# A running log-sum-exp on one core: carry by a VectorE shuffle, own-row sums on GpSimd, nine matmuls a tile, a pipeline one stage deeper

## The chip, the core and the metric

The kernel runs on one core of a Trainium2 chip. The metric is device time in microseconds (us), the median of several executions. Most agree within 0.3% (one slow one is left out).

In these kernels TensorE does the matmuls, ScalarE (ACT in the profile) the exponentials and logarithms, VectorE (DVE) and GpSimd (POOL) the sums. The tiles lie in SBUF; the matmuls write to PSUM. SyncE (SP) issues the transfers. Each transfer is split over 16 DMA engines. In a line of a timeline the first two numbers are start and duration in us, and the bracket at the end gives the wait before it and what ended it.

## The reference

The input x is 4 x 4096 x 4128 in fp32. Along the second axis the output is a running log-sum-exp:

```
out[:, 0] = x[:, 0]
for t in 1..4095:
    mx = max(out[:, t-1], x[:, t])
    out[:, t] = mx + log(exp(out[:, t-1] - mx) + exp(x[:, t] - mx))
```

Both kernels compute exp(x), a running sum, and the logarithm of it.

## The kernel before

A tile is 128 partitions x 3 consecutive rows x 4128 columns (6.34 MB); 4096 rows are ten tiles of three rows and one of two, 44 tiles in all. The first batch starts with its two-row tile, the others end with theirs. A tile arrives by one load, is worked on in place, and leaves by one store. There are four tile buffers. The columns are worked on in four chunks of 1024 (the last takes the remaining 32 too):

```
own:        row j += row j-1, j = 1, 2                      (VectorE)
head:       above += excl^T @ row 2   (sums of the partitions above)   (TensorE)
add_above:  all rows += above         (PSUM operand)        (VectorE)
pick:       above = last partition's last row, for the next tile       (TensorE)
...
for g, k in enumerate(chunks):
    if g + 1 < len(chunks):
        chunks[g + 1].own();  chunks[g + 1].head()
    if g + 2 < len(chunks):
        chunks[g + 2].act(ACT.Exp)
    if g:
        finish(chunks[g - 1]);  result(chunks[g - 1])       # Ln; after the last chunk: store(s), load(s + 3)
    k.add_above()
    ...                                                     # pick
```

ScalarE takes its work in the order in which this loop issues it, so the place of `act(Exp)` says how far ahead ScalarE runs.

The softmax here doesn't subtract the row's maximum and nothing guards it: scores larger than these inputs give would overflow.

## Time and profile before

| | before |
|---|---|
| median time | 1263.7 us (1263.48 to 1264.46) |
| span of the profiled run | 1266.3 us |
| VectorE / ScalarE / TensorE / GpSimd busy | 981 / 924 / 760 / 1 us |
| one 6.34 MB store, issue to landing | 27.0 us |
| one 6.34 MB load, issue to landing | 41.1 us |

The profiled run was a slow one of its kind: other runs of this kernel have spans of 1261.7 to 1264.1, so differences taken from its trace are about 4 us too small. The two latencies are in the last column of the list of transfers:

```profile
xt<-in_x_dram SPq DMA_DIRECT2D x40, 6192.0 KB, 41.1
out_dram<-xt SPq DMA_DIRECT2D x40, 6192.0 KB, 27.0
```

What exceeds the transfer's own time is time in the queue.

### The profile page before, as it was taken

How to read it: one execution, taken by the hardware profiler on the slowest of the kernel's cores; microseconds unless marked ns; L12 is line 12 of the kernel's file. 1: busy time of each engine (PE TensorE's matmuls, PEld its weight loads, DVE VectorE, ACT ScalarE, POOL GpSimd, SP SyncE). 2: the span in 40 equal slices, each digit the busy share in tenths (PEclk: the TensorE clock that was granted, in tenths of full speed). 3: DMA queues.
4: the chain of work that ended last, by engine and by line, in shares of the span. 5: the costliest groups of instructions: out<-in, count | busy, mean ns of one | idle time of the engine just before them, and what ended most of it. 6: DMA issues, size and time to landing. Idle time of an engine off the chain costs nothing.

```text
span 1266.3 us, 4623 instructions
## 1 busy us (share of the span) xinstructions
PE 760.5 (60%) x1512; PEld 289.0 (23%) x1512; DVE 980.6 (77%) x597; ACT 923.8 (73%) x353; POOL 1.1 (0%) x8
## 2 busy tenths in 40 slices
PE   4676665555666666666366666665646656666562
PEld 1222222222222222222122222222212222222220
DVE  3998777777777878788579878777857978787793
ACT  4887666777777777767668777666866877766794
POOL 0000000000000000000000000000000000000000
PEclk9998888887788888888779888888877988888886
DMA  9999999999999999999999999999999999999998
GB/s 409 384 425 424 427 429 443 426 427 440 432 429 441 426 430 440 429 431 433 434 434 434 429 440 430 431 437 433 432 419 434 426 433 433 431 432 438 426 418 349
DMA packets 12695, 541.35 MB, mean 427 GB/s; under 512 B 1409, under 2 KB 1409, under 8 KB 1409
## 3 DMA queue, kind: packets, MB, share of 16 engines
q1 hardware_dynamic: 12672, 541.07, 99.3%
q8 instruction: 12, 0.20, 0.1%
q14 instruction: 11, 0.08, 0.0%
HBM read 270.53 MB, written 270.53 MB: 427 GB/s over the span
## 4 chain that ended last, share of the span: by engine, by line
DMA 67%; DVE 12%; ACT 9%; PE 8%; issue 1%; SPq 0%; ACTq 0%
DMA xt<-in_x_dram 63%; DVE xt L77 12%; ACT xt L106 9%; PE above L74 8%; DMA out_dram<-xt 5%; SPq L97 0%; ACTq L106 0%; SPq L94 0%; DVE carry_t L146 0%
## 5 line engine op out<-in xcount | busy, mean ns | idle before, releaser
L106 ACT ACTIVATE xt<-xt 128x3072 f32<-128x3072 f32 (+2 forms) x352 | 922.5, 2693 | 327.0 <-DMA xt<-in_x_dram 290.5
L74 PE MATMUL above<-xt,excl 128*128 128x512 f32 (+1 forms) x792 | 443.1, 687 | 348.7 <-DVE xt L77 339.4
L77 DVE TENSOR_TENSOR xt<-xt 128x1024 f32<-128x1024 f32 (+1 forms) x336 | 413.4, 1230 | 255.0 <-ACT xt L106 249.4
L77 DVE TENSOR_TENSOR xt<-xt,above 128x3072 f32<-128x3072 f32 (+3 forms) x220 | 582.9, 2651 | 11.7 <-PE above L74 10.3
L74 PE MATMUL above<-xt,pick 128*128 128x512 f32 x640 | 330.7, 630 | 130.0 <-DVE xt L77 130.0
L74 PEld LDWEIGHTS above<-xt,excl 128*128 128x128 f32 x792 | 162.6, 229 | 601.5 <-issue 490.5
L74 PEld LDWEIGHTS above<-xt,pick 128*128 128x128 f32 x640 | 113.6, 198 | 307.4 <-DVE xt L77 227.2
L74 PEld LDWEIGHTS above<-carry_t,pick 128*128 128x128 f32 x80 | 20.8, 271 | 51.4 <-DVE xt L77 48.2
L74 PE MATMUL above<-carry_t,pick 128*128 128x32 f32 x80 | 17.5, 308 | 10.1 <-DVE xt L77 10.1
L146 DVE COPY carry_t<-xt 32x32 f32<-32x32 f32 x40 | 7.1, 178 | 1.4
L56 ACT ACT_TABLE_LOAD x1 | 1.3, 1283 | 0.8 <-PEq L214 0.8
L69 DVE MEMSET carry_t<- 128x32 f32 x1 | 0.1, 85 | 0.9 <-PEq L214 0.9
L27 POOL TENSOR_SCALAR_AFFINE_SELECT pick<-pick 128x128 f32<-128x128 f32 x1 | 0.3, 293 | 0.0
L21 POOL TENSOR_SCALAR_AFFINE_SELECT excl<-excl 128x128 f32<-128x128 f32 x1 | 0.3, 292 | 0.0
L19 POOL MEMSET excl<- 128x128 f32 x1 | 0.2, 204 | 0.3 <-POOLq L214 0.3
L26 POOL MEMSET pick<- 128x128 f32 x1 | 0.2, 204 | 0.0
L214 POOL MEMSET const-bfloat16-1.0<- 128x1 bf16 x1 | 0.1, 101 | 0.0
L214 POOL MEMSET const-uint8-127<- 128x1 uint8 x1 | 0.1, 101 | 0.0
L214 POOL MEMSET const-float32-0.0<- 128x1 f32 x1 | 0.1, 98 | 0.3 <-issue 0.3
L214 POOL MEMSET const-float32-1.0<- 128x1 f32 x1 | 0.1, 98 | 0.0
## 6 DMA issues: line engine op xcount, KB each, us to landing
xt<-in_x_dram SPq DMA_DIRECT2D x40, 6192.0 KB, 41.1
out_dram<-xt SPq DMA_DIRECT2D x40, 6192.0 KB, 27.0
xt<-in_x_dram SPq DMA_DIRECT2D x4, 4128.0 KB, 36.2
out_dram<-xt SPq DMA_DIRECT2D x4, 4128.0 KB, 19.6
```

The costliest lines, as they stand in the source:

```text
L19: nc.gpsimd.memset(excl, 1.0)
L21: nc.gpsimd.affine_select(out=excl, in_=excl, pattern=[[1, P]], compare_op=mybir.AluOpType.is_ge, fill=0.0, base=-1, channel_multiplier=-1,)
L26: nc.gpsimd.memset(pick, 0.0)
L27: nc.gpsimd.affine_select(out=pick, in_=pick, pattern=[[0, P]], compare_op=mybir.AluOpType.not_equal, fill=1.0, base=-(P - 1), channel_mul ...
L56: nc.scalar.preload_act_table_set("natural_log_exp_and_others")
L69: nc.vector.memset(carry_t, 0.0)
L74: nc.tensor.matmul(pt, lhsT=w, rhs=rhs, start=start, stop=stop, skip_group_check=True)
L77: nc.vector.tensor_tensor(out=o, in0=a, in1=b, op=mybir.AluOpType.add)
L106: nc.scalar.activation(v, v, func)
L146: nc.vector.tensor_copy(carry_t[96:, :], t.xt[96:, t.r - 1, t0:D])
L214: nc = _bacc.Bacc("TRN2", target_bir_lowering=False, num_devices=1)
```

## The change

Its intent: take work off TensorE and VectorE. The last row's sum goes by a shuffle on VectorE into a small `carry` and is added to the next tile's first row (`begin`), so the `pick` matmuls and the accumulation in PSUM fall away. GpSimd does the own-row sums. The pipeline gets one stage deeper, four loads are issued at the start, and the last tile runs by itself after all others are done. The diff, cut:

```
+    carry = [psum.tile([Q, CH], ...)] + [cpool.tile([Q, ...]) for c in 1..3]      # Q = 32
+        def begin(self):
+            if not t.first:
+                nc.vector.scalar_tensor_tensor(out=v, in0=carry[c], scalar=one, in1=v, mult, add)
         def own(self):
-                add(v, x[:, j - 1, a:b], v)
+                add(nc.gpsimd, v, x[:, j - 1, a:b], v)
+        def end(self):
+            if not t.final:
+                nc.vector.stream_shuffle(carry[c], t.xt[P - Q:, t.r - 1, a:b], [Q - 1] * Q)
...
-    for s in steps[:ahead]:
+    for s in steps[:bufs]:
         s.load()
...
+    for part in (steps[:-1], steps[-1:]):
+        ...
+        for g in range(-3, N + 1):
+            chunks[g + 3].act(ACT.Exp)
+            chunks[g + 2].begin();  chunks[g + 2].own()
+            chunks[g + 1].head()
+            result(chunks[g - 1])                            # Ln, store, load
+            chunks[g].add_before();  chunks[g].end()
```

More of the change, by code (lines that the diff above doesn't have):

```diff
@@ L13 @@
 MM = 512
+Q = 32
 def _constants(nc, pool):
@@ L24, in _constants @@
     )
-    pick = pool.tile([P, P], FP32, name="pick")
-    nc.gpsimd.memset(pick, 0.0)
+    one = pool.tile([Q, 1], FP32, name="one")
+    nc.gpsimd.memset(one, 0.0)
     nc.gpsimd.affine_select(
-        out=pick, in_=pick, pattern=[[0, P]], compare_op=mybir.AluOpType.not_equal,
-        fill=1.0, base=-(P - 1), channel_multiplier=1,
+        out=one, in_=one, pattern=[[0, 1]], compare_op=mybir.AluOpType.not_equal,
+        fill=1.0, base=0, channel_multiplier=1,
     )
-    return excl, pick
+    return excl, one
 @with_exitstack
@@ L50 @@
     assert S % P == 0
-    n_main = D // CH
-    tail = D - n_main * CH
-    t0 = n_main * CH
-    last = n_main - 1
+    NC = D // CH
+    tail = D - NC * CH
+    t0 = NC * CH
+    last = NC - 1
     nc.scalar.preload_act_table_set("natural_log_exp_and_others")
     consts = ctx.enter_context(tc.tile_pool(name="consts", bufs=1))
-    excl, pick = _constants(nc, consts)
+    excl, one = _constants(nc, consts)
     bufs = 4
@@ L62, with add @@
     cpool = ctx.enter_context(tc.tile_pool(name="cpool", bufs=1))
+    hpool = ctx.enter_context(tc.tile_pool(name="hpool", bufs=2, space=bass.MemoryType.PSUM))
     psum = ctx.enter_context(tc.tile_pool(name="psum", bufs=1, space=bass.MemoryType.PSUM))
-    above = [psum.tile([P, CH], FP32, name=f"above{c}") for c in range(n_main)]
-    above_t = above[last][:, CH - MM:CH - MM + tail]
-    carry_t = cpool.tile([P, tail], FP32, name="carry_t")
-    nc.vector.memset(carry_t, 0.0)
+    carry = [psum.tile([Q, CH], FP32, name="carry0")]
+    carry += [cpool.tile([Q, CH if c < last else D - last * CH], FP32, name=f"carry{c}")
+              for c in range(1, NC)]
     ctx.enter_context(tc.manual_schedule())
-    def mm(pt, w, rhs, start=False, stop=False):
-        nc.tensor.matmul(pt, lhsT=w, rhs=rhs, start=start, stop=stop, skip_group_check=True)
-    def add(o, a, b):
-        nc.vector.tensor_tensor(out=o, in0=a, in1=b, op=mybir.AluOpType.add)
+    def add(eng, o, a, b):
+        eng.tensor_tensor(out=o, in0=a, in1=b, op=mybir.AluOpType.add)
     class Step:
@@ L106, in act @@
             nc.scalar.activation(v, v, func)
+        def begin(self):
+            t = self.t
+            if not t.first:
+                v = t.xt[:Q, 0, self.a:self.b]
+                nc.vector.scalar_tensor_tensor(
+                    out=v, in0=carry[self.c], scalar=one, in1=v,
+                    op0=mybir.AluOpType.mult, op1=mybir.AluOpType.add,
+                )
         def own(self):
@@ L112, in own, with add_before @@
                 v = x[:, j, self.a:self.b]
-                add(v, x[:, j - 1, self.a:self.b], v)
+                add(nc.gpsimd, v, x[:, j - 1, self.a:self.b], v)
         def head(self):
-            t, a = self.t, self.a
-            for s in range(0, CH, MM):
-                mm(above[self.c][:, s:s + MM], excl, t.xt[:, t.r - 1, a + s:a + s + MM],
-                   start=t.first, stop=True)
-        def add_above(self):
-            t, a = self.t, self.a
-            v = t.xt[:, :, a:a + CH]
-            add(v, v, above[self.c].unsqueeze(1).to_broadcast([P, t.r, CH]))
-        def pick(self, s0=0, s1=CH):
-            t, a = self.t, self.a
-            if not t.final:
-                for s in range(s0, s1, MM):
-                    mm(above[self.c][:, s:s + MM], pick, t.xt[:, t.r - 1, a + s:a + s + MM],
-                       start=True)
-        def tail_head(self):
-            t = self.t
-            if not t.first:
-                mm(above_t, pick, carry_t, start=True)
-            mm(above_t, excl, t.xt[:, t.r - 1, t0:D], start=t.first, stop=True)
-        def tail_add(self):
-            t = self.t
-            v = t.xt[:, :, t0:D]
-            add(v, v, above_t.unsqueeze(1).to_broadcast([P, t.r, tail]))
-            if not t.final:
-                nc.vector.tensor_copy(carry_t[96:, :], t.xt[96:, t.r - 1, t0:D])
+            t = self.t
+            e = t.xt[:, t.r - 1, self.a:self.b]
+            self.pt = hpool.tile([P, CH], FP32, name="pt")
+            parts = [(self.pt[:, s:s + MM], e[:, s:s + MM]) for s in range(0, CH, MM)]
+            if self.c == last:
+                self.qt = psum.tile([P, tail], FP32, name="qt")
+                parts.append((self.qt, e[:, CH:]))
+            for o, v in parts:
+                nc.tensor.matmul(o, lhsT=excl, rhs=v, start=True, stop=True)
+        def add_before(self):
+            t = self.t
+            parts = [(t.xt[:, :, self.a:self.a + CH], self.pt)]
+            if self.c == last:
+                parts.append((t.xt[:, :, t0:], self.qt))
+            for v, p in parts:
+                add(nc.vector, v, v, p.unsqueeze(1).to_broadcast(v.shape))
+        def end(self):
+            t = self.t
+            if not t.final:
+                nc.vector.stream_shuffle(
+                    carry[self.c], t.xt[P - Q:, t.r - 1, self.a:self.b], [Q - 1] * Q,
+                )
     steps = []
@@ L158 @@
         assert row == S
-    chunks = [Chunk(s, c) for s in steps for c in range(n_main)]
     ahead = bufs - 1
-    for s in steps[:ahead]:
+    for s in steps[:bufs]:
         s.load()
     stored = 0
-    def finish(k):
-        if k.c == last:
-            k.tail_add()
-            k.pick(CH - MM)
     def result(k):
@@ L174, in result @@
             k.t.store()
-            if stored + ahead < len(steps):
+            if bufs <= stored + ahead < len(steps):
                 steps[stored + ahead].load()
             stored += 1
-    chunks[0].act(ACT.Exp)
-    chunks[1].act(ACT.Exp)
-    chunks[0].own()
-    chunks[0].head()
-    for g, k in enumerate(chunks):
-        if g + 1 < len(chunks):
-            chunks[g + 1].own()
-            chunks[g + 1].head()
-        if g + 2 < len(chunks):
-            chunks[g + 2].act(ACT.Exp)
-        if g:
-            finish(chunks[g - 1])
-            result(chunks[g - 1])
-        k.add_above()
-        if k.c == last:
-            k.tail_head()
-            k.pick(0, CH - MM)
-        else:
-            k.pick()
-    finish(chunks[-1])
-    result(chunks[-1])
+    for part in (steps[:-1], steps[-1:]):
+        chunks = [Chunk(s, c) for s in part for c in range(NC)]
+        N = len(chunks)
+        for g in range(-3, N + 1):
+            if 0 <= g + 3 < N:
+                chunks[g + 3].act(ACT.Exp)
+            if 0 <= g + 2 < N:
+                chunks[g + 2].begin()
+                chunks[g + 2].own()
+            if 0 <= g + 1 < N:
+                chunks[g + 1].head()
+            if 0 <= g - 1:
+                result(chunks[g - 1])
+            if 0 <= g < N:
+                chunks[g].add_before()
+                chunks[g].end()
 _INS = ['x']
```

## The prediction

> **What bounds the kernel now.** I began with the page's slices and queues.
>
> ```profile
> DMA  9999999999999999999999999999999999999998
> GB/s 409 384 425 424 427 429 443 426 427 440 432 429 441 426 430 440 429 431 433 434 434 434 429 440 430 431 437 433 432 419 434 426 433 433 431 432 438 426 418 349
> ...
> q1 hardware_dynamic: 12672, 541.07, 99.3%
> ```
>
> The DMA row has no gap, and the queue's packets fill 99.3% of 16 engines' span. 541.07 MB is the input once and the output once, and the change moves the same bytes. Next, busy time by stretch, with three places where the slices dip:
>
> ```profile
> 100.00:1230.00 1130.00, 685.11 (x1355) 260.38 (x1356) 886.22 (x538) 832.26 (x314) 0.00 (x0) 0.87 1.00 432
> ...
> 42.00:100.00 58.00, 42.39 (x88) 15.40 (x86) 55.66 (x34) 49.00 (x19) 0.00 (x0) 0.94 0.98 401
> 42.00:44.50 2.50, 2.00 (x6) 0.72 (x5) 2.47 (x3) 2.50 (x2) 0.00 (x0) 1.00 0.50 211
> ...
> 1241.00:1266.30 25.30, 4.02 (x8) 1.70 (x8) 5.96 (x4) 7.97 (x5) 0.00 (x0) 0.59 0.89 386
> ```
>
> The last two columns are the DMA share and GB/s. Between 100 and 1230 us the rate is a flat 432; 541.07 MB at 432 is 1252.5 us. The span of 1266.3 is thus only about 14 us above a stream without a gap: some 4 us in 42 to 100 (58 x (1 - 401/432), with the hole at 42 in it), some 3 us at the start (403 GB/s over the first 42 us), the rest at the end.
>
> Then I asked how much slack feeds the stream: the timeline of the DMA-issuing queue and of ScalarE.
>
> ```profile
> 385.53 0.34 SPq L97 DMA_DIRECT2D out_dram<-xt  x1
> 385.96 0.38 SPq L94 DMA_DIRECT2D xt<-in_x_dram  x1
> 415.31 0.34 SPq L97 DMA_DIRECT2D out_dram<-xt  x1
> 415.75 0.38 SPq L94 DMA_DIRECT2D xt<-in_x_dram  x1
> ```
> ```profile
> 368.68 13.38 ACT L106 ACTIVATE xt<-xt 128x3072 f32<-128x3072 f32 x5 [7.11 <-DMA xt<-in_x_dram]
> 382.66 8.23 ACT L106 ACTIVATE xt<-xt 128x3168 f32<-128x3168 f32 x3 [0.61 <-PE above L74]
> ```
>
> A load lands, ScalarE wakes at 368.68, and the store of the tile before goes out at 385.53: C = 16.9 us from landing to next issue. With the store goes one load. Such a pair is 2 x 6.34 MB, so at 432 GB/s 29.4 us of transfer, which is the step between the pairs. A pair issued C after a landing finds 29.4 - 16.9 = 12.5 us still queued. The page agrees: its stores land a median 27.0 us after issue, 12.3 more than the 14.7 one takes. So C may grow by some 12 us before the stream starves, and shrinking it gains nothing.
>
> **What the Trainium skill says.** "DMA: Bandwidth & Descriptors", section Where 436 GB/s comes from, gives a ceiling of 435.2 GB/s for the 16 ports. The 432 over 1130 us agrees, so there is no rate to win. "GPSIMD Engine Reference", section 3.1, has the fp32 tensor_tensor add of 2048 elements at 4497 ns on GpSimd against 2293 on VectorE. The trace has VectorE's 1024 at 1222 ns, which fits; it has no such GpSimd work, so 2.3 us for 1024 is an estimate (half of 4497, rounded up). "VectorE: DVE Perf Modes", the perf-mode tier table, has the shuffle at one element a cycle, about 2400 ns for 2048: an estimated 1.2 us for 1024. "SBUF — State Buffer", section SBUF: two separate sides, says that a VectorE operation with two SBUF inputs and a GpSimd operation that reads SBUF exclude each other for whole instructions. No run yet shows that; nothing ran on GpSimd.
>
> **The change part by part.** From the groups by shape:
>
> ```profile
> L106 ACT ACTIVATE xt<-xt 128x3072 f32<-128x3072 f32 x240 | 645.9, 2750 | 273.0 <-DMA xt<-in_x_dram 273.0
> ...
> L77 DVE TENSOR_TENSOR xt<-xt,above 128x3072 f32<-128x3072 f32 x160 | 535.7, 3348 | 1.2
> ...
> L77 DVE TENSOR_TENSOR xt<-xt 128x1024 f32<-128x1024 f32 x252 | 308.1, 1222 | 248.3 <-ACT xt L106 244.0
> ```
>
> VectorE loses 336 own-row adds (413.4 us on the page) and the 40 small copies (7.1). It gains 160 adds of the carry into row 0 (32x1024, estimate 1.22, as a 1024 add: 195 us) and 160 shuffles (1.2: 192 us). 980.6 - 420.5 + 387 = 947 us: hardly less. GpSimd gets 336 x 2.3 = 773 us, 61% of the span. TensorE drops from 1512 matmuls to 44 x 9 = 396; at about 0.65 us for a 512-wide one it goes from 760 to some 250 us busy. ScalarE keeps 923. None reaches the span, so the stream stays the bound if C stays below 29.4.
>
> New C: exponentials now run three chunks ahead instead of two, so ScalarE does four exponentials and four logarithms between the landing and the store: 8 x 2.75 = 22 us. Do the others keep up? A chunk needs its carry add on VectorE (1.22), then two GpSimd adds (4.6), beside which VectorE does the add of the prefix (3.35) and a shuffle (1.2), 4.55. In three of four chunks the carry lies in SBUF, so the next carry add has two SBUF inputs and must wait for GpSimd: a chunk takes 1.22 + 4.6 + about 0.4 for handing over, 6.2 us, a tile 25 us. Under 29.4, and C stays 22, since the logarithm that ends it belongs to a chunk whose row sums were done before the landing. Queued at an issue: 29.4 - 22 = 7.4 us instead of 12.5. **In steady state the change buys and costs nothing.**
>
> Start: four loads go out at once, not three, which fills the hole at 42 (about 1.3 us lost: 2.5 x (1 - 211/432), near 2 us by packets). But ScalarE, behind since 27.7 us, sends the second store at about 27.7 + 4 x 4.65 + 22 = 68.3 or a little later, while four loads and the first store end near 4 x 14.7 - 4 + 10 + 2 = 67. A hole of the same kind moves there. I book -1 us.
>
> End: this is where the kernels differ. The chain of waits shows before's last tile:
>
> ```profile
> 1226.15 1.92 ACT xt L106
> ...
> 1246.34 2.30 DVE xt L77
> ...
> 1249.67 1.96 ACT xt L106
> ```
>
> The last load lands at 1226, its exponentials run while the tile before is finished, and the last store is issued at 1251.7, 4 us before the one ahead of it has gone out (the trace's landings: 1255.8, then 1265.5). So before's end is transfer. After drains the last-but-one tile before it starts the last. From its landing (1201.7) that tile needs 22 us, then two more rounds of row sums, prefix and logarithm, about 15: near 1238. Only then the last tile's exponentials: 1.9 + 1.2 for the first carry add, four chunks of GpSimd (2.3 each, with a 1.2 us carry add between, as the two exclude each other: 12.8), matmuls 2.2, add 2.5, logarithm 2: 22.6 us. Last store at about 1260.5, 9.8 us of transfer, then the 1 us that before has too: about 1271.5, +5 us. Without the exclusion 3.6 us less: +1.5.
>
> Sum: 1263.6 - 1 + 4 (between +1.5 and +5, nearer the upper) = 1266.6; I say 1266.
>
> **Rivals.** (a) GpSimd becomes the bound. Two adds and a carry add per chunk exceed 29.4/4 = 7.35 us if one add takes over 2.9 us. At 3.3 us with hand-over 0.4 a tile takes 4 x (1.22 + 6.6 + 0.4) = 33 us, 44 tiles about 1440. For it: no GpSimd add in the trace, only an estimate. Against: it would have to be 26% slower than the page's figure. (b) The exclusion reaches further than I think. If shuffles also shut GpSimd out, a chunk is 1.22 + 4.6 + 1.2 + 0.4 = 7.4 us, on the edge: 1270 to 1290. If every VectorE add does, it is above 10 us and the kernel above 1750. Against: the prefix add has one input in PSUM. (c) Freed VectorE, and TensorE no longer on the path, speed it up. The chain gives them 20% of the span, but the DMA row is full beside it: that chain is one thread of a closed loop whose spare 12 us show as queueing. Even with both dips removed it would be 1250 to 1255, inside 2%. (d) The end costs nothing, because the drained pipeline lets the last-but-one store go earlier: 1262.
>
> **Range and chances.** With the stream the bound, the time lies between 1258 (start and end both better) and 1277 (the exclusion at the end in full, its terms 5 us too small). For (a) and (b) together I give about 10% of being over 1289. Faster by over 2% means below 1238, under the 1252.5 of the stream itself: 1%.
>
> **What would show it.** Right: DMA still 9s everywhere, 432 GB/s from 100 to 1230, stores landing about 22 us after issue instead of 27, some 22 us from a landing to the next store, GpSimd near 770 us with adds of 2.3 us, and the loss in the last 40 us with a gap in the transfers before the last store. Wrong: 8s or less in the middle of the DMA row, ScalarE waiting for VectorE or TensorE instead of loads, GpSimd adds of 3 us or more, carry adds stretched far over 1.2 us, or a last store issued before 1252.

## The result, and the profile after

The changed kernel took 1294.78 us (1290.85 to 1295.14), 31 us more. The ratio is 1.0238, 95% interval 1.0217 to 1.0258. Ratios here are the mean time of one kernel's fast runs over that of the other's in the same rounds, so not quite the ratio of the medians. The forecast of 1266, with a range up to 1277, was wrong.

The page of the changed kernel, with its slices and its queue:

```profile
DMA  9999999999999999999999999999999999999987
GB/s 405 422 383 414 427 437 431 428 440 432 425 440 431 426 435 420 433 426 388 400 443 405 425 420 439 437 423 438 384 422 441 397 417 439 434 423 440 430 346 302
...
q1 hardware_dynamic: 12672, 541.07, 98.0%
```

The DMA row still looks full, but the row below it does not. The kernel before has one such dip near the start too (384; here 383) and one in its last slice (349). New are 388, 384 and 397 in the middle and 346 and 302 at the end. Busy time by stretch of the changed kernel (start and end, length, then PE, PEld, DVE, ACT and POOL; last three columns: granted TensorE clock, DMA share, GB/s):

```profile
594.00:602.00 8.00, 5.63 (x7) 1.85 (x6) 7.91 (x6) 5.85 (x3) 6.07 (x3) 0.50 0.65 279
42.00:100.00 58.00, 35.64 (x44) 11.97 (x44) 57.20 (x40) 47.51 (x18) 45.61 (x20) 0.59 0.95 388
100.00:1200.00 1100.00, 513.63 (x675) 179.99 (x676) 850.55 (x602) 792.98 (x301) 693.01 (x293) 0.61 0.99 425
1271.00:1284.00 13.00, 4.67 (x11) 1.80 (x10) 7.31 (x5) 6.46 (x4) 2.43 (x1) 0.76 0.33 142
```

The same question to the kernel before:

```profile
594.00:602.00 8.00, 6.04 (x13) 2.41 (x14) 7.85 (x6) 5.92 (x3) 0.00 (x0) 1.00 1.06 456
100.00:1200.00 1100.00, 666.59 (x1318) 253.00 (x1318) 861.17 (x522) 806.80 (x304) 0.00 (x0) 0.87 1.00 432
```

So 1100 us of stream went from 432 to 425 GB/s: the same bytes take 18 us longer. Around 594 to 602 us the engines move 279 GB/s where they moved 456. And near the end there are 13 us at 142.

Was it an engine that became the bound? The groups by shape say no:

```profile
L78 POOL TENSOR_TENSOR xt<-xt 128x1024 f32<-128x1024 f32 x252 | 596.2, 2367 | 421.9 <-DVE xt L114 368.4 <-ACT xt L107 44.1
L136 PE MATMUL pt<-xt,excl 128*128 128x512 f32 x704 | 590.4, 988 | 676.0 <-POOL xt L78 664.9 <-DVE xt L78 10.3 <-issue 0.8
...
L114 DVE SCALAR_TENSOR_TENSOR xt<-carry,one,xt 32x1024 f32<-32x1024 f32 x120 | 159.1, 1326 | 211.8 <-ACT xt L107 209.1
...
L149 DVE STREAM_SHUFFLE carry<-xt 32x1024 f32<-32x1024 f32 x120 | 152.4, 1270 | 1.6
```

A GpSimd add takes 2.37 us (2.3 had been estimated), a carry add 1.33 and a shuffle 1.27 (1.22 and 1.2). Only TensorE is far off: 600 us busy instead of 250. Its lines on the two pages, before and after:

```profile
PE 760.5 (60%) x1512; PEld 289.0 (23%) x1512; DVE 980.6 (77%) x597; ACT 923.8 (73%) x353; POOL 1.1 (0%) x8
PE 600.5 (46%) x792; PEld 210.1 (16%) x792; DVE 990.9 (77%) x700; ACT 920.9 (71%) x353; POOL 800.1 (62%) x344
```

The page lists two records for each matmul call: 792 for the 44 x 9 = 396 calls of the changed kernel, 1512 for 756 before. The forecast multiplied calls by the time of one record. On top of that a 512-wide record takes 988 ns at a granted clock of 0.62, not 650. All engines still wait often. The time from a landing to the next store is also as forecast. A load's last engine lands at 400.02; then ScalarE and the issuing queue:

```profile
400.05 21.50 ACT L107 ACTIVATE xt<-xt 128x3072 f32<-128x3072 f32 x8 [7.79 <-DMA xt<-in_x_dram]
```
```profile
421.57 0.33 SPq L98 DMA_DIRECT2D out_dram<-xt  x1
422.00 0.38 SPq L95 DMA_DIRECT2D xt<-in_x_dram  x1
```

Eight ScalarE instructions, 21.5 us, then the store: C, the time from landing to store, is 21.5 us where 22 was predicted. The queue shrank as predicted too:

```profile
xt<-in_x_dram SPq DMA_DIRECT2D x40, 6192.0 KB, 37.3
out_dram<-xt SPq DMA_DIRECT2D x40, 6192.0 KB, 22.8
```

What the forecast had not asked is whether all 16 DMA engines have that queue. The trace records when each of them finishes its share of a transfer. Here are first and last engine around the first inner two-row tile:

| transfer | before: first to last engine, us | after: first to last engine, us |
|---|---|---|
| load of tile 20 | 568.6 to 573.6 | 571.9 to 578.3 |
| store of tile 18 | 583.3 to 588.3 | 587.2 to 592.9 |
| load of tile 21 (two rows) | 593.0 to 598.0 | 597.0 to 602.7 |
| store of tile 19, issued at 590.6 / 599.9 | 607.7 to 612.6 | 616.3 to 618.1 |
| load of tile 22 | 622.5 to 627.2 | 631.9 to 634.4 |

In both kernels the engines are 5 to 6 us apart. Before, the store of tile 19 comes 2.4 us before the first engine has emptied its queue. After, it comes 2.8 us too late for that engine, and 2.8 us before the last one would be empty. The fast engines stop, and when all run again the next two transfers take the last engine 15.4 and 16.3 us instead of 14.6. How far the last engine of the changed kernel is behind that of the kernel before:

| by the landing of | us behind |
|---|---|
| store of tile 3 | 1.6 |
| store of tile 18 | 4.6 |
| load of tile 22, two transfers after the short load | 7.1 |
| load of tile 25, after the short store | 9.9 |
| store of tile 41 | 16.7 |
| store of tile 42 | 18.2 |
| store of tile 43, the last | 26.6 |

So two losses: some 17 us up to the store of tile 41, and 10 us in the last two transfers. About 8 of the 17 come around the two-row tiles 21 and 32. Much of the rest builds up at stores that found every engine with 1 us or more still queued.

The queue's line gives another cut. Its share times the span is the time of the packets, per engine: 98.0% of 1292.9 us is 1267 us, where the kernel before has 99.3% of 1266.3, 1257 us. So the engines stand idle for 17 us more, and the packets themselves take 10 us longer. Of the packets' part nearly all lies between the stores of tiles 3 and 41 (9 us, with 6 us of idle time beside it). "Starved" is thus only a part of the loss of the middle; why the packets ran longer was not found. The loss of the last two transfers comes from the order at the end. The last load lands at 1242.8, but ScalarE takes up that tile only at 1257.8, when the tile before is drained. The last store:

```profile
1280.92 0.33 SPq L98 DMA_DIRECT2D out_dram<-xt  x1
```

The store before it had landed at 1274.0, so the engines stood idle for some 8 us (last packet done at 1273.6, next one at 1281.8), 0.8 of it after the issue.

### The profile page after: what moved, and what is told of

It reads as the page before. It is cut to its first block, busy times and chain, and to the rows that moved or that the text cites. A ratio compares the mean times of both kernels' runs of the same rounds, so it can differ in the third digit from the quotient of the medians.

```text
span 1292.9 us, 3961 instructions
## 1 busy us (share of the span) xinstructions
PE 600.5 (46%) x792; PEld 210.1 (16%) x792; DVE 990.9 (77%) x700; ACT 920.9 (71%) x353; POOL 800.1 (62%) x344
## 4 chain that ended last, share of the span: by engine, by line
DMA 57%; ACT 23%; DVE 9%; issue 8%; POOL 1%; PE 1%; SPq 1%; ACTq 0%; DVEq 0%
DMA xt<-in_x_dram 57%; ACT xt L107 23%; DVE xt L78 5%; DVE xt L114 2%; DVE carry L149 2%; POOL xt L78 1%; PE pt L136 1%; SPq L98 0%; ACTq L107 0%; SPq L95 0%; DVEq L78 0%; DVEq L221 0%; DVEq L114 0%
## 5 line engine op out<-in xcount | busy, mean ns | idle before, releaser
L107 ACT ACTIVATE xt<-xt 128x3072 f32<-128x3072 f32 (+3 forms) x352 | 919.6, 2691 | 359.2 <-DMA xt<-in_x_dram 340.1
L78 POOL TENSOR_TENSOR xt<-xt 128x1024 f32<-128x1024 f32 (+1 forms) x336 | 799.3, 2380 | 473.2 <-DVE xt L114 415.9
L136 PE MATMUL pt<-xt,excl 128*128 128x512 f32 x704 | 590.4, 988 | 676.0 <-POOL xt L78 664.9
L78 DVE TENSOR_TENSOR xt<-xt,pt 128x3072 f32<-128x3072 f32 (+1 forms) x176 | 569.7, 3239 | 66.0 <-PE pt L136 57.0
L114 DVE SCALAR_TENSOR_TENSOR xt<-carry,one,xt 32x1024 f32<-32x1024 f32 (+1 forms) x160 | 217.2, 1358 | 212.9 <-ACT xt L107 209.1
L136 PEld LDWEIGHTS pt<-xt,excl 128*128 128x128 f32 x704 | 183.0, 286 | 1024.6 <-POOL xt L78 865.0
L149 DVE STREAM_SHUFFLE carry<-xt 32x1024 f32<-32x1024 f32 (+1 forms) x160 | 206.0, 1287 | 2.1
L136 PEld LDWEIGHTS qt<-xt,excl 128*128 128x128 f32 x88 | 27.1, 308 | 41.6 <-issue 41.6
L136 PE MATMUL qt<-xt,excl 128*128 128x32 f32 x88 | 18.7, 303 | 0.0
L78 DVE TENSOR_TENSOR xt<-xt,qt 128x96 f32<-128x96 f32 (+1 forms) x44 | 10.2, 233 | 0.0
## 6 DMA issues: line engine op xcount, KB each, us to landing
out_dram<-xt SPq DMA_DIRECT2D x40, 6192.0 KB, 22.8
out_dram<-xt SPq DMA_DIRECT2D x4, 4128.0 KB, 21.6
```

Source lines behind the costliest of these rows:

```text
L78: eng.tensor_tensor(out=o, in0=a, in1=b, op=mybir.AluOpType.add)
L107: nc.scalar.activation(v, v, func)
L114: nc.vector.scalar_tensor_tensor(out=v, in0=carry[self.c], scalar=one, in1=v, op0=mybir.AluOpType.mult, op1=mybir.AluOpType.add,)
L136: nc.tensor.matmul(o, lhsT=excl, rhs=v, start=True, stop=True)
L149: nc.vector.stream_shuffle(carry[self.c], t.xt[P - Q:, t.r - 1, self.a:self.b], [Q - 1] * Q,)
```

## The experiments

The edits shown are cut and their names shortened. There is no e7.

**Theories.** The feed theory: the later store (C of 21.5 us instead of 16.9) leaves too little queued; some DMA engines run empty; that costs the 17 us, and the separate last tile costs the 10. The GpSimd theory: work on GpSimd, the ports it shares with VectorE, or the lower TensorE clock slow the chain of a chunk.

**e1, logarithm first.** The changed kernel; ScalarE's order alone is altered.

```
+            result(chunks[g - 1])        # Ln, store, load
             chunks[g + 3].act(ACT.Exp)
...
-            result(chunks[g - 1])
```

> The changed kernel with one reordering: ScalarE does the logarithm of a finished chunk before, not after, the exponential three chunks ahead. From a landing to the next store there are then three exponentials and three logarithms, 16.5 us, as in the kernel before, instead of 22; GpSimd, VectorE and TensorE do exactly what they did. Feed theory (the late store leaves too little queued, some DMA engines run empty, and that loses the 16.7 us that build up before the last two transfers): those 16.7 us go, the 10 us at the end stay: 1279 us (1274 to 1283), and no starved stretch in the middle. GpSimd theory (row sums on GpSimd, the ports it shares with VectorE, or the lower TensorE clock slow the chain of a chunk): nothing of that changes: 1293 to 1296.

It took 1283.38 us, 11 less; a smaller gain than expected. C fell to 17.9, not 16.5: the logarithm now waits for the shuffle that reads the row it overwrites, as the waits show (us in total, times, longest):

```profile
ACT xt L107 <- DVE carry L149: 60.8, 87, 4.6
```

The lag behind the kernel before at the store of tile 41 is 6.6 us instead of 16.7; the last two transfers still add 9.4. So 10 of the 17 us go when ScalarE's order alone is changed, with GpSimd busy for the same 800 us.

**e2, one pipeline.** The changed kernel without the separate last tile.

```
-    for part in (steps[:-1], steps[-1:]):
+    for part in (steps,):
```

> The changed kernel with all tiles in one pipeline: the last tile is no longer held until the one before it is done. Drain theory of the end: the last two transfers lose their 10 us against the kernel before; here the last tile's exponentials run as it lands, the store before it goes out some 19 us after that landing, and the last store follows without the 8.4 us gap: 1288 us (1285 to 1291). Rival: the end is long because GpSimd and VectorE exclude each other and the TensorE clock is low, which stays: within 2 us of the changed kernel.

It took 1288.23 us, as the drain theory has it. The lag at the store of tile 41 stays, 14.6 us; the last two transfers add 4.6 instead of 9.9.

**e4, the kernel before with exponentials three chunks ahead.** No GpSimd, no shuffle.

```
-        if g + 2 < len(chunks):
-            chunks[g + 2].act(ACT.Exp)
+        if g + 3 < len(chunks):
+            chunks[g + 3].act(ACT.Exp)
...                                      # and chunks[2].act(ACT.Exp) before the loop
```

> The kernel before with only its exponentials moved to three chunks ahead; nothing on GpSimd, no shuffle, 18 matmuls a tile as before. Feed theory: from a landing to the next store 22 us instead of 16.9, stores landing about 22 us after issue, engines that run empty at the short tiles, and the same slow build-up: 1280 us (1274 to 1288). GpSimd or clock theory: no change, 1264 (1262 to 1266).

It took 1282.07 us: 18 us lost by one move in ScalarE's order. C is 21.5, stores land 22.4 us after issue, and the stream in the middle is down although the TensorE clock is 0.86:

```profile
100.00:1200.00 1100.00, 655.28 (x1304) 248.55 (x1305) 851.75 (x518) 799.64 (x303) 0.00 (x0) 0.86 1.00 428
```

In its trace the same starved places appear, near 595, 913, 1232 and 1248 us. Its queue's line has both parts of the loss as well, 8 us more idle and 7 us more of packets (1264 us of 1280.5) than the kernel before:

```profile
q1 hardware_dynamic: 12672, 541.07, 98.7%
```

The GpSimd and clock theories, which expected 1264, can't make this loss.

**e5, the kernel before with the own-row sums on GpSimd.**

```
-                add(v, x[:, j - 1, a:b], v)
+                nc.gpsimd.tensor_tensor(out=v, in0=x[:, j - 1, a:b], in1=v, op=add)
```

> The kernel before with only its own-row sums moved to GpSimd. Feed theory: the wait from a landing to the next store stays near 17 us, so no change: 1264 us (1262 to 1267), with GpSimd near 800 us busy. GpSimd theory: much of the loss appears: 1275 to 1295.

It took 1274.42 us, against the expectation of the feed theory. But that rested on C staying near 17, and C was 19.0. So this run did not tell the theories apart; e15 and, in part, e16 do.

**e3, the changed kernel with the edits of e1 and e2.**

> The changed kernel with both edits so far: logarithm first, and one pipeline for all tiles. If the late store and the held last tile are separate losses, the gains add: 1283.4 (logarithm first alone) less the 6.6 that one pipeline took off: 1277 us (1274 to 1280). If one loss hides the other, it stays above 1281.

It took 1277.12 us: the two losses are separate and add.

**e6, the kernel before with the logarithm first.**

```
+        if g:
+            finish(chunks[g - 1]);  result(chunks[g - 1])
         if g + 2 < len(chunks):
             chunks[g + 2].act(ACT.Exp)
-        if g:
-            finish(chunks[g - 1]);  result(chunks[g - 1])
```

> The kernel before with the logarithm of a finished chunk ahead of the exponential. From a landing to the next store about 11.6 us instead of 16.9. Feed theory: where nothing starves more queueing is worth nothing in the middle; only the first holes shrink: 1261 us (1258 to 1264). If the margin still cost something in the kernel before, it would fall further, below 1258.

It took 1337.15 us, a miss of 76 (the record's median, 1339.17, has the slow execution in it). ScalarE now waits on the chain of a chunk:

```profile
ACT xt L106 <- PE above L74: 355.8, 87, 8.2
```

In the kernel before that wait was 33.9 us. With the logarithm of one chunk ahead of the exponential of the third, only two chunks are in flight, and sums, matmuls and the prefix of one must end before ScalarE may go on. Too shallow a pipeline loses here far more than too deep a one.

**e8, the same with four loads at the start.**

```
-    for s in steps[:ahead]:
+    for s in steps[:bufs]:
...                                      # and no load after the first store
```

> As the logarithm-first form of the kernel before, with four loads issued at the start instead of three, as in the changed kernel. The hole of 2 us at 42 us goes and, with the earlier second store, does not move to 67 us: 1259 us (1256 to 1263). If the hole only moves, the same time as with three loads.

1339.22 us: the stall of e6 hides whatever the fourth load does, so nothing follows.

**e9, e6 with the own-row sums on GpSimd** (the edit of e5).

> The kernel before with own-row sums on GpSimd and the logarithm first. With the sums on GpSimd alone it took 1274.4, and the wait from a landing to the next store had grown from 16.9 to 19.0 us. Feed theory: the loss is that growth, and here the wait falls to about 15.5 us, so: 1264 us (1261 to 1267). If GpSimd's work itself slows the kernel, it stays above 1270.

1504.32 us, a miss of the same kind: the chain that ScalarE waits for is longer by the slower adds (536.8 us of waiting for TensorE). It says nothing on the feed.

**e10, the kernel before, three ahead and the logarithm first** (the edits of e4 and e6). This completes a square of depth and order.

> The kernel before with exponentials three chunks ahead and the logarithm first. Exponentials three ahead alone took 1282.1 and the logarithm first alone 1339.2. If the first lost by a late store (landing to store 21.5 us) and the second by a chain with too few chunks in flight, each mends the other: landing to store about 17 us, nothing stalled: 1265 us (1262 to 1269). If the two losses have other causes they add up: above 1282.

1264.03 us, ratio 0.9999 (0.9984 to 1.0014).

| kernel before | exponential first | logarithm first |
|---|---|---|
| two ahead | 1263.7 (C 16.9) | 1337.2 |
| three ahead | 1282.1 (C 21.5) | 1264.0 (C 16.9) |

Its stream in the middle:

```profile
100.00:1200.00 1100.00, 664.00 (x1318) 251.11 (x1318) 860.41 (x522) 808.70 (x305) 0.00 (x0) 0.87 1.00 433
```

Depth itself costs nothing here. What costs is the late store, and the order repairs it.

**e11, e10 with the own-row sums on GpSimd** (the edit of e5).

> As the run beside it (kernel before, three ahead, logarithm first), with the own-row sums on GpSimd. Feed theory: with landing to store at about 17 us GpSimd's 800 us of work cost nothing: 1266 us (1262 to 1270), within 4 us of the run without GpSimd. GpSimd theory: 8 us or more above it, as the sums on GpSimd alone were 10.6 above the kernel before.

1275.57 us, again against the feed theory's number, and again with C at 19.0. The timeline shows why: ScalarE's last logarithm of a tile waits for a pick matmul, which stands behind a chunk whose sums GpSimd ends later than VectorE did. GpSimd's slower sums thus cost time in e5 and e11, by way of C; e16 tests this:

```profile
415.14 8.23 ACT L106 ACTIVATE xt<-xt 128x3168 f32<-128x3168 f32 x3 [2.64 <-PE above L74]
```

**e16, e11 with the tail of a finished chunk (the last sum and the pick) ahead on VectorE and TensorE.**

```
+        if g:
+            finish(chunks[g - 1])
         if g + 1 < len(chunks):
             chunks[g + 1].own();  chunks[g + 1].head()
         if g:
-            finish(chunks[g - 1])
             result(chunks[g - 1])
```

> As the run with three ahead, logarithm first and the sums on GpSimd (1275.6), with one reordering on TensorE: the tail of a finished chunk goes before the next chunk's prefix matmuls, for which ScalarE's last logarithm waited 2.6 us a tile. From a landing to the next store about 17 us instead of 19.0. Feed theory: GpSimd cost only through that wait, so 1266 us (1263 to 1269). GpSimd theory (its work or its port slows the kernel by itself): it stays above 1272.

1268.13 us. The wait halved, C fell to 17.6, and 7.4 of e11's 12 us over the kernel before went with it, GpSimd still busy for 800 us:

```profile
412.94 8.23 ACT L106 ACTIVATE xt<-xt 128x3168 f32<-128x3168 f32 x3 [1.23 <-PE above L74]
```

**e15, e4 with the own-row sums on GpSimd** (the edit of e5), at an equal C.

> The kernel before with exponentials three ahead (1282.1 alone) and the own-row sums on GpSimd. Landing to store is 21.5 us in both, set by ScalarE. Feed theory: the same time, 1283 us (1280 to 1286). If GpSimd's work adds a loss of its own at an equal wait, as the 6 us between this family and the changed kernel in one pipeline (1288.2) could suggest: 1287 or more.

1283.77 us against 1282.07 without GpSimd, C 21.6 and 21.5. At an equal C the GpSimd work costs nothing that can be told from noise.

**e12, the changed kernel with stores in two halves of the columns.** No compute engine's instructions change.

```
+        if k.c == 1:
+            k.t.store(0, 2 * CH)
         if k.c == last:
-            k.t.store()
+            k.t.store(2 * CH, D)
```

> The changed kernel with each tile's store in two halves of the columns, the first half issued when the second chunk's logarithm is done. No engine's instructions change, only the transfers' issue: half a store goes out some 11 us earlier, so the engines have some 7 us more queued. Feed theory: most of the 16.7 us of the middle go, and some of the gap of 8.4 us before the last store: 1277 us (1272 to 1283). Theories in which compute engines slow each other: no change, 1293 to 1296; if the shorter rows of the split cost transfer rate, above that.

1283.64 us, 11 less, just outside the range. Until about 1240 us its trace has no starved stretch left. **e13** is the kernel before with the same edit.

> The kernel before with the same split of each store. In the middle nothing starves, so nothing is won there; the holes at 42 and 67 us are filled by the first halves: 1260 us (1256 to 1264). If the split costs transfer rate, above 1268.

1276.00 us, slower by 12: the first holes were filled as expected (422 GB/s from 42 to 100 us), but with the shorter rows the rate in the rest is lower. The middle of e12, then of e13:

```profile
100.00:1200.00 1100.00, 525.10 (x681) 182.52 (x680) 857.45 (x607) 798.55 (x303) 698.87 (x295) 0.61 1.01 428
```
```profile
100.00:1200.00 1100.00, 663.24 (x1309) 252.03 (x1307) 856.32 (x520) 806.39 (x304) 0.00 (x0) 0.86 1.01 429
```

So e12 paid the rate too and won by more than the 11 us show. With the queue kept full both kernels stream alike, whether GpSimd works or not and at either TensorE clock.

**e14, the kernel before with only the first two tiles' stores split.**

```
+        if k.c == 1 and stored < 2:
+            k.t.store(0, 2 * CH)
         if k.c == last:
-            k.t.store()
+            k.t.store(2 * CH if stored < 2 else 0, D)
```

> The kernel before with the store in two halves for the first two tiles only. With all stores split the stretch from 42 to 100 us ran at 422 GB/s instead of 401, and the rest lost rate to the shorter rows; here only the gain is kept: about 2.8 us, 1261 us (1259 to 1263). If the slow stretch only moves to the tiles after, 1264.

1262.36 us (1262.17 to 1262.97), ratio 0.9984 (0.9971 to 0.9998). The stretch after the start is now full:

```profile
42.00:100.00 58.00, 42.11 (x88) 15.50 (x86) 56.19 (x34) 49.88 (x20) 0.00 (x0) 0.94 1.01 427
```

It beats both kernels. Its gain over the kernel before, 0.16%, is clear of noise by the interval but far below 2%.

**All runs by C.** "Queued" is how long after the issue of a store the first and the last engine would have run empty (medians of the trace).

| kernel | C, us | queued: first / last engine, us | time, us |
|---|---|---|---|
| before | 16.9 | 7.5 / 12.4 | 1263.7 |
| e10 | 16.9 | 7.8 / 12.4 | 1264.0 |
| e16 (GpSimd) | 17.6 | 7.0 / 11.3 | 1268.1 |
| e5 (GpSimd) | 19.0 | 6.4 / 10.3 | 1274.4 |
| e11 (GpSimd) | 19.0 | 6.3 / 10.3 | 1275.6 |
| e4 | 21.5 | 4.1 / 7.7 | 1282.1 |
| e15 (GpSimd) | 21.6 | 4.3 / 7.7 | 1283.8 |
| e3 (changed, both edits) | 17.9 | 6.9 / 11.4 | 1277.1 |
| e2 (changed, one pipeline) | 21.6 | 4.0 / 8.0 | 1288.2 |
| after | 21.5 | 3.9 / 8.1 | 1294.8 |

Within the kernel before and its variants the time follows C, with or without GpSimd. Two limits: the only pair with and without GpSimd at an equal, longer C is e4 and e15, since all runs between 16.9 and 21.5 have GpSimd in them; and not all of the loss is in the steady stream. By the landings 4 of the 8 us that e5's trace has over e10's, and 7 of e4's 17, lie before the store of tile 3 (the hole at 42 us grew) and in the last two transfers. By the queue's lines the packets' time grows with C along with the idle time: 1256 us in e10 and 1257 in the kernel before, 1259 in e5, 1264 in e4 and 1266 in e2.

The changed kernel's variants lie above that row: e2 by 4 us over e15, e3 by 9 over e16. That remainder stays open. The start is not it: by the store of tile 3, e2 is 1 us ahead of e15 and e3 1 us ahead of e16. The shuffle and the carry adds were not tried by themselves.

## Why the prediction was wrong, point by point

- **The bound** was right. The stream of transfers sets the time in every variant but e6, e8 and e9.
- **Instruction costs** were right except TensorE's. GpSimd 800 us on the page (773), VectorE 991 (947); TensorE 600 instead of 250. There the prediction set 396 calls against the page's 1512 records, two for a call, and so lost a factor of two; and it took the old matmul's duration. The Trainium skill, "TensorE: Matmul & The Clock Gate", Part 1, says that an idle TensorE is throttled to half its clock; the trace agrees in direction (busy 46% and granted 0.62 after, 60% and 0.87 before). It did not decide: e4 lost 18 us at a clock of 0.86. "GPSIMD Engine Reference", section 3.1, held: 2.37 us for 1024 elements beside 4.50 stated for 2048.
- **New C of 22 us** was right: 21.5. Stores landing 22 us after issue: 22.8.
- **"In steady state the change buys and costs nothing"** is the step that failed. Its 7.4 us of queue is a figure for the last engine and for pairs of three-row transfers (measured 8.1). It left out two things. The engines are some 2 to 7 us apart, so the first has 3.9 us in the median. And a pair with a two-row tile in it is only some 24 us of transfer, so there the last engine has 2.8 us and the first is already empty (-2.8 at the worst). Both were in the trace before: a spread of 5 us, and at the short tiles only 0.5 to 2.6 us left to the first engine. The mean was right and the minimum decided. The prediction also took it that no cost comes before a queue is empty, and that a starved moment costs that moment only. But the two transfers after one were up to 2.5 us slower together as well, and over the whole run the packets took 10 us longer, beside 17 us of idle engines. With this step falls the sentence that C may grow by some 12 us before the stream starves: 4.6 us more of C cost 18 us in e4.
- **The end** had the right mechanism and the wrong size: up to +5 worked out, +4 booked, +9.9 in the trace, of which e2 gave back 6.6 us of measured time (5.3 of it in the last two transfers). From the last tile's first exponential to its last store it took 23.1 us (22.6 predicted). But the drain before it was too short in the forecast: from the landing of tile 42 (1218.4) to that exponential (1257.8) it was 39.4 us, not 36.3, because ScalarE's last three logarithms each waited 2 to 2.8 us for VectorE's shuffle. And the last store took 11.2 us to land, not 9.8, since the engines had stopped.
- **The exclusion of GpSimd and VectorE** was right in its mechanism and small in effect. In the last tile:

```profile
1259.74 1.27 DVE L114 SCALAR_TENSOR_TENSOR xt<-carry,one,xt 32x1024 f32<-32x1024 f32 x1 [4.79 <-ACT xt L107]
1261.54 4.23 DVE L114 SCALAR_TENSOR_TENSOR xt<-carry,one,xt 32x1024 f32<-32x1024 f32 x2 [0.53 <-ACT xt L107]
```

  The first carry add takes 1.27 us; the next two, with GpSimd's add running from 1261.14 to 1263.49, take 4.23 together (3.03 and 1.27 in the records). Over the whole kernel the mean is 1.33 us. So this bears out "SBUF — State Buffer", section SBUF: two separate sides. e15 has no carry adds and so does not test it; but C is 21.5 us in the changed kernel as in e4, where GpSimd does nothing, so it did not delay the stores of the steady stream. Its share in the end was not tried by itself.
- **The start** was booked at -1 us and cost +1.6 by the store of tile 3: the hole moved to 67 us, as said there, and was larger (3.4 us of idle engines after, 1.9 before).
- **The rivals**: neither (a) nor (b) came true, and both were given the whole chance of a loss. The one that did was not on the list: a full-looking queue that some engines empty. Of the others, neither (c), a gain, nor (d), an end that costs nothing, came true.

## What to carry to other kernels

When a transfer stream is the bound, the slack to read is not the mean time in the queue but what the earliest of the DMA engines still has queued at the smallest transfers; read that from the landings per engine before calling a later store free. Making a pipeline deeper moves stores later in program order: with the store's last instruction placed ahead of the new stage's, the depth was free here (1264.0 us), and behind it the same depth cost 18 us. A last tile that is held until the others are drained puts its whole latency at the end.

## What the Trainium skill lacked or had wrong

- "DMA: Bandwidth & Descriptors", section Latency and other measured facts, has two engines as usually slower in traces, but not by how much. Here the first and the last engine are 0.5 us apart in the first load of the kernel before and 7.0 us by the store of tile 40. There not two but five of the 16 trail, by 4.6 us or more; the others land within 1.5 us.
- The same page has nothing on what follows when some engines run empty under load: after such a moment the next two transfers took 15.4 and 16.3 us in the changed kernel, where most take 14.6 to 14.7. Why was not found.
- The same page, section Why small descriptors are slow, puts the penalty at descriptors of some hundred bytes. With rows of 8 KB instead of 49.5 KB on the store side the rate was about 1% lower here (429 against 432 to 433 GB/s).
